# One minimum for both halves of the keys in a softmax, and the division by its sums moved to the gate of the output

## The chip, the cores and the metric

The kernel runs on one core of a Trainium2 chip. The metric is the device time of one execution in microseconds (us); the number given for a kernel is the median of its runs. Beside it stands one execution taken with the hardware profiler, from which all rows below come.

## What is computed

One layer of a bidirectional encoder in float32, for a prompt of 1024 tokens ("p" in the names of tiles) and a sample of 512 ("s"). After a combined input projection two groups of eight heads work side by side: a gated delta rule (group A, a scan in both directions) and a dense attention (group B). Both are multiplied by a gate, put side by side and go through the output projection. The change touches the attention alone:

```python
s = jnp.einsum('bhqd,bhkd->bhqk', qi, k) * MLA_SCALE     # query and key: 128 columns + 64 rotated ones
p = jax.nn.softmax(s, axis=-1)                           # over all positions
o_b = jnp.einsum('bhqk,bhkd->bhqd', p, v)
mix = jnp.concatenate([o_a * jax.nn.silu(z_a), o_b * jax.nn.silu(z_b)], axis=-1)
y = jnp.einsum('bse,ed->bsd', mix, w_out)
```

## The kernel before

Matmuls take float32 operands that are split into a rounded high part and a low part; a product is then three matmuls (high by high, high by low, low by high). `split` (its lines 196 and 199 in the profile) makes the two parts: ScalarE copies the high one, VectorE or POOL subtracts for the low one.

TensorE's order is written out by hand. Every part of the program is a generator that issues some matmuls, adds their estimated time to a clock (`cost`) and yields the time from which it wants to go on. `merge` always lets the first stream go on whose time has come: the three streams of the delta rule (scan, back, front) first, then the main stream, then one that may fill gaps. When none is ready, the clock jumps ahead. The times steer only the order; on the chip TensorE runs that order as fast as operands and buffers allow. The order on the other engines and on SP's DMA queue is found by the compiler's own simulation, beforehand.

In the stretch from 2137 us the main stream is `attention`, first for the prompt, then for the sample. The delta rule's last heads run beside it; when they are done, products of the output projection (`first`, lines 1151 to 1153) may fill gaps. All streams before that end earlier.

`attention` goes over eight heads, for each over blocks of 256 queries. `keys` makes the head's keys, `scores` the scores of one block, `pair_values` the values of two heads. The keys lie in halves of 512: two halves for the prompt (`nh` = 2), one for the sample (`nh` = 1). `scores` takes 128 queries at a time (loop over `i`) and, for each half, writes five matmuls (lines 1013 to 1017) into one of two banks (tile `s`). VectorE finds the minimum of the half (line 1020, the scores are negated), ScalarE the exponential with its sum (line 1021). After the second half the two are brought to a common minimum: a factor for each half, the sum of both, its reciprocal (lines 1029 to 1033), and POOL multiplies the probabilities `pe` by the factor (line 1035). With one half it is a reciprocal (line 1026) and the multiplication. After each half `scores` yields.

`values` works on an earlier block, 256 keys at a time: TensorE transposes the probabilities into the one bank `pt` (line 1074), ScalarE and VectorE split it into `pth` and `ptl` (lines 196 and 199), and `pv` multiplies the parts of the step before by the values into the one bank `po` (lines 1051 to 1053). At the last step of a block VectorE multiplies `po` by the gate `z` (line 1056), and the result goes to DRAM. Between two steps of `values` the planner leaves `PLAT` = 2.0 of its time; `beside` calls one step of `values` after each yield of `scores`, `keys` or `pair_values`, and starts the next half `SLAT` = 3.0 after the one before the last ended.

## Time and profile before

| | |
|---|---|
| median of 3 runs | 3327.83 us (3327.79 to 3335.36) |
| profiled execution | 3330.34 us, span 3328.5 us |
| busy over the span | TensorE 3166.2 us (95%), VectorE 1739.8, ScalarE 1282.5, POOL 1154.3 |
| granted TensorE clock, mean | 0.985 |
| attention over the prompt | 2137 to 2683 us |
| attention over the sample | 2683 to 2850 us |

The span runs from the first to the last instruction. PE is TensorE's matmuls, PEld its weight loads (which run beside the matmuls of the instruction before), DVE is VectorE, ACT ScalarE, POOL GpSimd, SP the queue that issues the DMAs. A busy time is a sum of rows; rows of TensorE overlap, since a matmul's row lasts until its last result is written while the next one has already begun. Idle time stands beside a group of instructions with the operations that ended it.

### The profile page before, as it was taken

What the parts mean: (1) busy time and instruction counts of PE and PEld (TensorE: products, weight loads), DVE (VectorE), ACT (ScalarE), POOL (GpSimd) and SP (SyncE); (2) the same over time, 40 slices, a digit from 0 to 9 for tenths busy, and PEclk for the clock granted to TensorE, in tenths of its full rate; (3) what the DMA queues carried; (4) which work ended last, traced back from release to release, by engine and by line L of the source; (5) the groups of instructions that cost most, each with busy time, mean ns of one, the idle gap of its engine ahead of it and who ended that gap; (6) DMA issues with size and microseconds to landing.
All of it is one profiled execution on the core that took longest, in us unless ns stands there. A gap on an engine that the chain in (4) does not pass through costs nothing.

```text
span 3328.5 us, 46972 instructions
## 1 busy us (share of the span) xinstructions
PE 3166.2 (95%) x16554; PEld 2628.6 (79%) x16554; DVE 1739.8 (52%) x4000; ACT 1282.5 (39%) x2956; POOL 1154.3 (35%) x1026
## 2 busy tenths in 40 slices
PE   8999999999999899999999988899999989999998
PEld 6888888888887678778788767688888878777876
DVE  7233334434411746765775576788787655330212
ACT  4222222222212334444345334365666555433231
POOL 6322222222222543332332333232223434454452
PEclk9999999999999899999999999999999999999999
DMA  4222222222222544434444466522322242564454
GB/s 160 84 70 74 78 73 80 71 79 80 86 73 73 179 119 123 120 107 137 130 109 127 137 209 210 160 82 59 102 77 79 90 134 86 159 189 134 145 171 133
DMA packets 271404, 381.66 MB, mean 115 GB/s; under 512 B 75632, under 2 KB 126824, under 8 KB 269632
## 3 DMA queue, kind: packets, MB, share of 16 engines
q1 hardware_dynamic: 271168, 378.66, 37.3%
q8 instruction: 130, 2.13, 0.3%
q14 instruction: 106, 0.87, 0.1%
HBM read 286.73 MB, written 88.29 MB: 113 GB/s over the span
## 4 chain that ended last, share of the span: by engine, by line
PE 28%; DVE 11%; DMA 7%; issue 3%; ACT 2%; POOL 2%; SPq 1%; POOLq 0%; DVEq 0%; ACTq 0%
DMA wraw<-w_out 3%; PE py L1152 3%; PE py L1151 3%; PE py L1153 3%; POOL wlo L199 2%; PE mm L224 2%; PE pt L1074 2%; PE mm L228 2%; PE mm L225 2%; DVE tm L737 2%; DVE XT L739 1%; PE po L1052 1%; PE po L1051 1%; PE po L1053 1%; PE Tp L791 1%
## 5 line engine op out<-in xcount | busy, mean ns | idle before, releaser
L199 POOL TENSOR_TENSOR wlo<-wraw,whi 128x512 fp32r<-128x512 f32 x620 | 831.7, 1345 | 1593.4 <-ACT whi L196 1476.3
L224 PE MATMUL mm<-hi,whi 128*128 128x512 f32 x2256 | 908.0, 404 | 21.8 <-ACT whi L196 16.3
L225 PE MATMUL mm<-lo,whi 128*128 128x512 f32 x2256 | 883.0, 393 | 8.1 <-DVE lo L255 8.1
L196 ACT ACTIVATE whi<-wraw 128x512 fp32r<-128x512 f32 x620 | 388.7, 631 | 1186.2 <-PE mm L225 695.8
L228 PE MATMUL mm<-hi,wlo 128*128 128x512 f32 x2256 | 765.5, 393 | 4.6 <-POOL wlo L199 4.6
L224 PEld LDWEIGHTS mm<-hi,whi 128*128 128x128 f32 x2256 | 428.1, 190 | 107.6 <-ACT whi L196 18.6
L228 PEld LDWEIGHTS mm<-hi,wlo 128*128 128x128 f32 x2256 | 426.5, 189 | 98.9 <-POOL wlo L199 7.2
L225 PEld LDWEIGHTS mm<-lo,whi 128*128 128x128 f32 x2256 | 427.9, 190 | 92.1 <-DVE lo L255 9.7
L1152 PE MATMUL py<-wlo,mhi 128*128 128x512 f32 x768 | 304.6, 397 | 8.1 <-POOL wlo L199 8.0
L1151 PE MATMUL py<-whi,mhi 128*128 128x512 f32 x768 | 303.7, 395 | 5.9 <-DVE y L1166 4.6
L1153 PE MATMUL py<-whi,mlo 128*128 128x512 f32 x768 | 303.1, 395 | 0.0
L1035 POOL TENSOR_TENSOR pe<-pe,af 128x512 f32<-128x512 f32 x160 | 166.6, 1058 | 373.2 <-DVE af L1033 189.9
L306 DVE SCALAR_TENSOR_TENSOR acc<-cin,conv_w,acc 128x1024 f32<-128x1024 f32 (+1 forms) x192 | 222.3, 1158 | 40.7 <-ACT acc L304 33.6
L302 DVE TENSOR_TENSOR cin<-mm,rbh 128x512 f32<-128x512 f32 x72 | 47.4, 687 | 310.0 <-PE mm L228 261.0
L1152 PEld LDWEIGHTS py<-wlo,mhi 128*128 128x128 f32 x768 | 145.2, 189 | 46.0 <-POOL wlo L199 14.6
L1151 PEld LDWEIGHTS py<-whi,mhi 128*128 128x128 f32 x768 | 145.2, 189 | 40.4 <-DVE y L1166 6.1
L1153 PEld LDWEIGHTS py<-whi,mlo 128*128 128x128 f32 x768 | 145.2, 189 | 32.3
L310 DVE TENSOR_TENSOR acc<-mm,rbh 128x512 f32<-128x512 f32 x48 | 31.6, 686 | 227.9 <-PE mm L228 227.6
L1166 DVE TENSOR_TENSOR y<-py,g 128x512 f32<-128x512 f32 x36 | 24.7, 689 | 239.3 <-ACT junk L1165 236.0
L1021 ACT ACTIVATE pe<-s,am 128x512 f32<-128x512 f32 x160 | 110.4, 690 | 89.1 <-DVE am L1020 78.5
L737 DVE TENSOR_TENSOR tm<-XT,lam 128x126 f32<-128x126 f32 (+22 forms) x372 | 131.2, 353 | 25.3 <-ACT lam L729 18.5
L199 DVE TENSOR_TENSOR ptl<-pt,pth 128x512 fp32r<-128x512 f32 x160 | 109.8, 686 | 52.7 <-ACT pth L196 51.8
(449 smaller groups left out, 5133.5 us busy)
## 6 DMA issues: line engine op xcount, KB each, us to landing
wraw<-w_in SPq DMA_DIRECT2D x376, 256.0 KB
wraw<-w_out SPq DMA_DIRECT2D x192, 256.0 KB
dd<-dX SPq DMA_DIRECT2D x48, 256.0 KB
wraw<-w_uq SPq DMA_DIRECT2D x36, 256.0 KB
x<-xT_p SPq DMA_DIRECT2D x16, 512.0 KB
xres<-x_p SPq DMA_DIRECT2D x8, 1024.0 KB
y_p<-y SPq DMA_DIRECT2D x32, 256.0 KB
x<-xT_s SPq DMA_DIRECT2D x16, 256.0 KB
```

The costliest lines, as they stand in the source:

```text
L196: nc.scalar.activation(hi, src, AF.Copy)
L199: (lo_eng or nc.vector).tensor_sub(lo, src, hi.bitcast(F32))
L224: nc.tensor.matmul(ps, whi[:, k], hi[:, s], start=kt == 0, stop=False)
L225: nc.tensor.matmul(ps, whi[:, k], lo[:, s], start=False, stop=False)
L228: nc.tensor.matmul(ps, wlo[:, k], hi[:, s], start=False, stop=kt == KT - 1)
L306: nc.vector.scalar_tensor_tensor(acc, cin[:, j:j + T], w[:, f, j:j + 1], acc, op0=ALU.mult, op1=ALU.add)
L737: nc.vector.tensor_mul(tv, XT[:, :m, j:j + 1].to_broadcast([P, m, n]), lam[j // 16][:, j % 16:j % 16 + 1, j + 1:].to_broadcast([P, m, n]))
L1021: nc.scalar.activation(pe[k], o, AF.Exp, bias=m[:, k:k + 1], scale=-1.0, accum_out=l[:, k:k + 1])
L1035: nc.gpsimd.tensor_mul(pe[k2], pe[k2], f[:, k2:k2 + 1].to_broadcast([P, BLK]))
L1151: nc.tensor.matmul(ps, hi[:, c], w[0], start=kt == kts[0], stop=False)
L1152: nc.tensor.matmul(ps, hi[:, c], w[1], start=False, stop=False)
L1153: nc.tensor.matmul(ps, lo[:, c], w[0], start=False, stop=kt == kts[1] - 1)
```

## The change

For the prompt, both halves of the scores are now written before anything else follows. The minimum of both halves goes into both exponentials, so that the halves need no factor. The probabilities stay undivided. Per block of 256 queries VectorE adds up the sums of the halves and takes the reciprocal; a DMA writes these 256 numbers to a row in DRAM, another reads the row back to all partitions (`rb`), and POOL multiplies the gate `z` by it before the gate is used. The planner gets a new constant `HLAT` = 2.4 after a pair of halves, and calls two steps of `values` after each pair (and after each yield of `keys` and `pair_values` for the prompt). For the sample, with one half, the order of `scores` and `values` stays.

```diff
@@ -29,6 +29,7 @@
 GAP = 8
 PLAT = 2.0
 SLAT = 3.0
+HLAT = 2.4
 
 
 QKV0, ZA0, CQ0, CKV0, ZB0, LAST = 0, 24, 32, 36, 38, 46
@@ -950,6 +951,7 @@
                     nc.vector.tensor_sub(krl[:64, ks], r[:64], krs[:64, ks].bitcast(F32))
         for h in range(H):
             self.dt(f"mix{8 + h}{q}", [P, T])
+        self.dt("rl" + q, [H, T])
 
         bank = lambda name: pss.tile([P, BLK], F32, tag="s", name=name, bufs=2)
 
@@ -987,7 +989,7 @@
                 yield
             out[:] = [vh, vl]
 
-        def scores(h, kh, kl, t0, pes):
+        def scores(h, kh, kl, t0, pes, rls):
             tq = slice(t0, t0 + QB)
             qn = ap.tile([P, QB], F32, tag="qn", name="qn")
             qp = ap.tile([P, QB], F32, tag="qp", name="qp")
@@ -1000,12 +1002,12 @@
             qr = ap.tile([P, QB], F32R, tag="qr", name="qr", bufs=2)
             nc.scalar.activation(qr, qp, AF.Copy)
             nc.vector.tensor_sub(qr[64:], qp[64:], qr[64:].bitcast(F32))
+            l = sm.tile([P, QB // P, nh], F32, tag="al", name="al", bufs=3)
+            rl = sm.tile([P, QB // P], F32, tag="ar", name="ar", bufs=4)
             for i in range(QB // P):
                 qs = slice(i * P, (i + 1) * P)
-                pe = []
+                pe, os = [], []
                 m = sm.tile([P, nh], F32, tag="am", name="am", bufs=4)
-                l = sm.tile([P, nh], F32, tag="al", name="al", bufs=4)
-                f = sm.tile([P, nh], F32, tag="af", name="af", bufs=4)
                 for k in range(nh):
                     ks = slice(k * BLK, (k + 1) * BLK)
                     pe.append(ap.tile([P, BLK], F32, tag="pe", name="pe", bufs=8 if nh > 1 else 6))
@@ -1016,25 +1018,27 @@
                     nc.tensor.matmul(o, qr[:, qs], krs[:, ks], start=False, stop=False)
                     nc.tensor.matmul(o, qr[:, qs], krl[:, ks], start=False, stop=True)
                     self.cost(BLK, 5)
+                    os.append(o)
 
                     nc.vector.tensor_reduce(m[:, k:k + 1], o, axis=AX.X, op=ALU.min)
-                    nc.scalar.activation(pe[k], o, AF.Exp, bias=m[:, k:k + 1], scale=-1.0,
-                                         accum_out=l[:, k:k + 1])
-                    if k == nh - 1:
-                        mm = sm.tile([P, 1], F32, tag="amm", name="amm", bufs=4)
-                        if nh == 1:
-                            nc.vector.reciprocal(f, l)
-                        else:
-
-                            nc.vector.tensor_tensor(mm, m[:, 0:1], m[:, 1:2], op=ALU.min)
-                            nc.scalar.activation(f, m, AF.Exp, bias=mm, scale=-1.0)
-                            nc.vector.scalar_tensor_tensor(l, l, 1.0, f, op0=ALU.mult, op1=ALU.mult, accum_out=mm)
-                            nc.vector.reciprocal(mm, mm)
-                            nc.vector.tensor_scalar(f, f, mm, None, op0=ALU.mult)
-                        for k2 in range(nh):
-                            nc.gpsimd.tensor_mul(pe[k2], pe[k2], f[:, k2:k2 + 1].to_broadcast([P, BLK]))
-                    yield
+                    if k < nh - 1:
+                        yield True
+                mm = m
+                if nh > 1:
+                    mm = sm.tile([P, 1], F32, tag="amm", name="amm", bufs=4)
+                    nc.vector.tensor_tensor(mm, m[:, 0:1], m[:, 1:2], op=ALU.min)
+                for k, o in enumerate(os):
+                    nc.scalar.activation(pe[k], o, AF.Exp, bias=mm, scale=-1.0, accum_out=l[:, i, k:k + 1])
                 pes.append(pe)
+                if i == QB // P - 1:
+
+                    src = l[:, :, 0]
+                    if nh > 1:
+                        nc.vector.tensor_reduce(rl, l, axis=AX.X, op=ALU.add)
+                        src = rl
+                    nc.vector.reciprocal(rl, src)
+                    rls.append(rl)
+                yield
 
 
         past, done, tick = [0.0, 0.0], [0.0], [0]
@@ -1046,12 +1050,17 @@
                 b["po"] = ps1.tile([P, QB], F32, tag="po", name="po")
                 b["z"] = ap.tile([P, QB], F32, tag="az", name="az", bufs=2)
                 nc.sync.dma_start(b["z"], S[f"f{ZB0 + b['h']}{q}"][:, b["tq"]])
+                nc.sync.dma_start(S["rl" + q][b["h"]:b["h"] + 1, b["tq"]].rearrange("a (i p) -> p (a i)", p=P), b["rl"][0])
             po, z = b["po"], b["z"]
             for j in range(2):
                 nc.tensor.matmul(po, vh[:, kb + j], hi[:, j], start=kb + j == 0, stop=False)
                 nc.tensor.matmul(po, vh[:, kb + j], lo[:, j], start=False, stop=False)
                 nc.tensor.matmul(po, vl[:, kb + j], hi[:, j], start=False, stop=kb + j == nt - 1)
             self.cost(2 * QB, 3)
+            if kb == 0:
+                rb = cp.tile([P, BLK], F32, tag="raw", name="rlb")[:, :QB]
+                nc.sync.dma_start(rb, S["rl" + q][b["h"]:b["h"] + 1, b["tq"]].to_broadcast([P, QB]))
+                nc.gpsimd.tensor_mul(z, z, rb)
             if kb + 2 == nt:
                 nc.vector.tensor_mul(z, po, z)
                 nc.sync.dma_start(S[f"mix{8 + b['h']}{q}"][:, b["tq"]], z)
@@ -1086,15 +1095,22 @@
             done[0] = self.t
 
         def beside(gen):
+            part = 0
             while True:
-                yield max(self.t, past[0] + SLAT)
+
+                yield self.t if part else max(self.t, past[1] + HLAT if nh > 1 else past[0] + SLAT)
                 try:
-                    next(gen)
+                    half = next(gen)
                 except StopIteration as e:
                     return e.value
                 past[:] = past[1], self.t
                 tick[0] += 1
+                part = part + 1 if half else 0
+                if part:
+                    continue
                 yield from values()
+                if nh > 1:
+                    yield from values()
 
         def finish():
             while queue or now[0] is not None or last[0] is not None:
@@ -1107,13 +1123,13 @@
                 wk = self.piece(a["w_uk"][h // 2], nc.gpsimd, ap, "2", 2, rb=3 - nh)
             kh, kl = yield from beside(keys(h % 2, wk))
             for t0 in range(0, T, QB):
-                pes = []
-                yield from beside(scores(h, kh, kl, t0, pes))
+                pes, rls = [], []
+                yield from beside(scores(h, kh, kl, t0, pes, rls))
                 if h % 2 == 0 and t0 == 0:
                     yield from finish()
                     wv = self.piece(a["w_uv"][h // 2], nc.gpsimd, ap, "2", 2, rb=3 - nh)
                     yield from beside(pair_values(wv, vs))
-                queue.append({"h": h, "tq": slice(t0, t0 + QB), "pes": pes, "tick": tick[0] + LAG,
+                queue.append({"h": h, "tq": slice(t0, t0 + QB), "pes": pes, "rl": rls, "tick": tick[0] + LAG,
                               "vs": [v[:, :, h % 2 * P:(h % 2 + 1) * P] for v in vs]})
         yield from finish()
```

## Rows read from the trace of the kernel before

**Rows 1.** The page: busy us of each engine, share of the span, instructions.

```profile
PE 3166.2 (95%) x16554; PEld 2628.6 (79%) x16554; DVE 1739.8 (52%) x4000; ACT 1282.5 (39%) x2956; POOL 1154.3 (35%) x1026
```

**Rows 2.** Stretches: length; busy us of PE, PEld, DVE, ACT, POOL; clock; DMA.

```profile
2137.00:2683.00 546.00, 512.53 (x3524) 445.96 (x3523) 424.34 (x1238) 325.95 (x910) 165.85 (x162) 0.99 0.28 84
2300.00:2500.00 200.00, 189.85 (x1400) 168.26 (x1399) 168.04 (x512) 120.77 (x354) 54.72 (x54) 1.00 0.27 80
```

**Rows 3.** Groups by line, 2137:2683: busy us, mean ns | idle before, releasers.

```profile
L1074 PE MATMUL pt<-ident,pe 128*128 128x128 f32 x512 | 80.0, 277 | 19.9 <-DVE ptl L199 10.2 <-DVE amm L1029 3.2 <-POOL pe L1035 2.4
L1074 PEld LDWEIGHTS pt<-ident,pe 128*128 128x128 f32 x512 | 59.6, 141 | 38.0 <-issue 12.4 <-DVE ptl L199 10.3 <-POOL pe L1035 4.4
L1013 PE MATMUL s<-kh,qh 128*128 128x512 f32 x128 | 54.4, 425 | 4.9 <-ACT pe L1021 2.6 <-DVE vl L199 2.3
L199 DVE TENSOR_TENSOR ptl<-pt,pth 128x512 fp32r<-128x512 f32 x128 | 87.8, 686 | 40.7 <-ACT pth L196 40.3
```

**Rows 4.** Timeline of PE, one half step alone: start us, us, instruction.

```profile
2497.67 0.40 PE L1013 MATMUL s<-kh,qh 128*128 128x512 f32 x1
...
2498.60 0.40 PE L1017 MATMUL s<-krl,qr 128*128 128x512 f32 x1
2498.84 0.60 PE L1074 MATMUL pt<-ident,pe 128*128 128x128 f32 x4
...
2499.99 0.39 PE L1013 MATMUL s<-kh,qh 128*128 128x512 f32 x1
```

**Rows 5.** Timeline of PE at a stalled transposition group (idle in brackets).

```profile
2404.42 0.40 PE L1017 MATMUL s<-krl,qr 128*128 128x512 f32 x1
2406.21 0.66 PE L1074 MATMUL pt<-ident,pe 128*128 128x128 f32 x4 [1.39 <-DVE ptl L199]
```

**Rows 6.** Groups by line, 2683:2850, the shorter attention.

```profile
L1074 PE MATMUL pt<-ident,pe 128*128 128x128 f32 x128 | 19.4, 274 | 2.2 <-DVE ptl L199 2.2
...
L1074 PEld LDWEIGHTS pt<-ident,pe 128*128 128x128 f32 x128 | 15.5, 140 | 7.8 <-DVE ptl L199 4.3
```

**Rows 7.** Groups by line, 2137:2683, operations that the change removes.

```profile
L1035 POOL TENSOR_TENSOR pe<-pe,af 128x512 f32<-128x512 f32 x128 | 132.6, 1057 | 322.7 <-DVE af L1033 189.9 <-PE pt L1074 22.5 <-DVE XT L739 14.9
L1030 ACT ACTIVATE af<-am,amm 128x2 f32<-128x2 f32 x64 | 19.2, 300 | 5.1 <-DVE amm L1029 4.5
L1033 DVE TENSOR_SCALAR af<-af,amm 128x2 f32<-128x2 f32 x64 | 15.3, 239 | 3.1 <-DVE XT L739 0.2
L1031 DVE SCALAR_TENSOR_TENSOR al<-al,af 128x2 f32<-128x2 f32 x64 | 11.0, 172 | 4.5 <-ACT af L1030 4.0
```

**Rows 8.** Timeline of POOL and DVE at one of the multiplications.

```profile
2401.68 2.04 POOL L1035 TENSOR_TENSOR pe<-pe,af 128x512 f32<-128x512 f32 x2 [7.43 <-PE s L1014]
2402.72 1.28 DVE L199 TENSOR_TENSOR ql<-qn,qh 128x256 fp32r<-128x256 f32 x1
```

**Rows 9.** Tile qn, whole span: duration ns min/median/max, first and last start.

```profile
L199 DVE TENSOR_TENSOR ql<-qn,qh x48: 411/425/1327, 2141.6 to 2816.8; 128x256 fp32r<-128x256 f32 x48
```

**Rows 10.** Timeline of DVE and ACT in the stretch of rows 4.

```profile
2499.04 0.69 DVE L1020 TENSOR_REDUCE am<-s 128x1 f32<-128x512 f32 x1 [0.23 <-PE s L1017]
2499.48 0.60 ACT L196 ACTIVATE pth<-pt 128x512 fp32r<-128x512 f32 x1 [1.72 <-PE pt L1074]
2499.97 0.68 ACT L1021 ACTIVATE pe<-s,am 128x512 f32<-128x512 f32 x1
2500.11 0.69 DVE L199 TENSOR_TENSOR ptl<-pt,pth 128x512 fp32r<-128x512 f32 x1 [0.38 <-ACT pth L196]
```

**Rows 11.** Timeline of PE: scores of half steps with no other work, first, last.

```profile
2180.07 0.40 PE L1013 MATMUL s<-kh,qh 128*128 128x512 f32 x1
...
2585.26 0.40 PE L1013 MATMUL s<-kh,qh 128*128 128x512 f32 x1
```

**Rows 12.** Chain of work that ended last: start us, us, landing of a write.

```profile
2159.57 1.89 DMA dUs<-UA
...
2680.70 1.73 DMA mix15p<-az
```

## Prediction

> **What bounds the kernel now.** I read first the page's busy times: TensorE is busy 95% of the span [rows 1], so a change that touches no matmul can only win back TensorE's waits. The question is how many lie where the change acts: the attention over the prompt (2137 to 2683 us) and the shorter one behind it (2683 to 2850). The table by stretches comes next: in the prompt attention TensorE is busy 512.5 of 546 us and VectorE 424.3, in its middle 168.0 of 200 [rows 2]. VectorE is the next to fill up.
>
> Third, the groups by line. TensorE's idle time ahead of the transpositions of the probabilities (tile pt, line 1074) is 19.9 us in its matmul row and 38.0 us in the row of its weight loads, of which 12.4 is put down to issue; the largest named releaser of both is VectorE's ptl (10.2 and 10.3). Ahead of the scores it is 4.9 us [rows 3]. The true figure lies between: a matmul of 512 columns has a row of 0.40 us but the next starts 0.23 us after it [rows 4], so a wait shows in the matmul row only when the pipeline has run dry. Counting in the timeline how much later than 0.23 us a transposition group starts, I get 28 us over the 128 groups, as at 2406.21 us, where 1.79 us lie between the starts and 1.56 are lost [rows 5]. In the shorter attention the same rows say 2.2 and 7.8 us [rows 6]; there I take 3. Everything that can be won at this spot is thus some 31 us, 0.9% of the time.
>
> **The change, part by part.** Taken away in the prompt attention: 128 POOL multiplications (132.6 us), 64 exponentials of the two-column factor on ScalarE (19.2 us), and on VectorE the product of sums and factors (11.0 us) and the scaling (15.3) [rows 7]. Of 64 reciprocals 32 stay, one per block of 256 queries, and with each comes a reduction of 4 columns to 2. The trace has none of that size; by the nearest row, two columns in 172 ns [rows 7], 32 cost 5.5 us, about what the 32 reciprocals save. So VectorE is relieved of some 11.0 + 15.3 = 26 us, 6% of its 424. POOL gets 48 multiplications of 128x256, half the width of those of 1057 ns: about 0.53 us each, 25 us over both attentions, on an engine that is busy 35% [rows 1]. None of this is on TensorE, so by itself it is worth nothing; it counts only where a wait of TensorE ends on VectorE or POOL.
>
> There is a second relief. At 2401.68 POOL runs two of the multiplications, 2.04 us; VectorE's ql takes 1.28 us beside them [rows 8], where its median is 425 ns [rows 9]. With POOL's 132.6 us gone most of this stretching goes too. I bound it from 0 to 30 us of VectorE time (128 times at most a quarter of a microsecond) and put VectorE's relief at 26 to 56 us, 6 to 13%.
>
> The order on TensorE changes as well. Before, each half of the scores is followed by a transposition group and a product group. After: both halves of the scores, then twice (transpositions, products), because the exponentials need the minimum of both halves. What follows for the single transposition buffer is read from a stretch without other work. One half step is 2.32 us: scores from 2497.67, transpositions from 2498.84, the next scores at 2499.99; transpositions and products take 1.15 us together [rows 4]. The transpositions of 2498.84 are copied by ScalarE from 2499.48 for 0.60 us, and ptl runs from 2500.11 for 0.69, done at 2500.80 [rows 10]. So the buffer is free 1.96 us after the group began. Before, the next group comes after 2.32 us, 0.36 to spare. After, the first group of a pair comes 1.15 + 2.33 = 3.48 us behind its predecessor, 1.5 to spare, the second only 1.15 us: it waits 1.96 - 1.15 + 0.04 (from ptl's end to the next matmul) = 0.85 us where nothing stands between. The planner puts 2.0 us of its own time between two such groups and fills them from the delta rule or the output projection; a scan item ready every 2.1 planned us is nearly always there. In the timeline 22 of 128 half steps hold nothing else, the first without a wait at 2180.07, the last at 2585.26 [rows 11], so I take 11 bare pairs (8 to 16).
>
> The sum for the prompt attention: of 28 us of waits the half before first groups goes, -14. The 53 covered second groups keep 14 x 53/64 = 11.6 less a quarter for VectorE's relief, 8.7; 11 bare ones cost 9.4 (7 to 14). Left are 18, gain 10. The 2.4 us that transpositions wait for POOL [rows 3] go.
>
> Against it: the next scores need a bank back. After the last matmul of a pair has begun come the second minimum (0.44 later, 0.69 long), the minimum of the two halves (two columns, 0.17) and the first exponential (0.68) [rows 4, 7, 10]: 1.98 us and two hand-overs of some 0.04. TensorE has meanwhile that matmul's 0.23 and two groups of 1.15, 2.5 us. It holds, by 0.5 us. Waits for a bank are 4.9 us now [rows 3]; I add 2 (0 to 6). Behind the first block of each second head the values' product follows a pair directly: four times up to 2 us, +1 (0 to 8).
>
> **The round trip of the sums.** Per block two DMAs come onto SP's queue: 256 sums of 4 bytes each to DRAM, then one row broadcast to all partitions, which waits for the first to land. The gate's multiplication on POOL waits for the second, behind it the low parts of weights, and VectorE's final product of the block waits for POOL. The nearest rows: a write of a block's result lands in 1.73 us, the 64 KB of dU, in 128-byte pieces, in 1.89 [rows 12]. Two landings and the multiplication are some 4.3 us, with two issues 5. From the products' first group, where the sums are issued at the latest, to the last there are three transposition groups, in the prompt attention some 9 us. Cover: those groups. Cost zero; without cover it would be the part beyond.
>
> The shorter attention (one half of keys) keeps its order, loses 32 POOL multiplications and 16 of 32 reciprocals: its 3 us of waits become 2, -1. Sum: -9.9 - 2.4 + 2 + 1 - 1 = -10.3 us. The span of 3328.5 becomes 3318.2; the profiled execution took 3330.3, 1.8 more than its span and 2.5 more than the median 3327.8. Against the median: 3327.8 - 10.3 = **3317.5 us**.
>
> **The rivals.** (a) *Slower: ScalarE takes the exponentials first.* The order of its queue is fixed beforehand. If the new exponential, ready 1.2 us after a pair, stands ahead of the copy of the first transposition group, ready at 0.65, the copy and with it ptl come a whole exponential (0.68) and the wait for it (0.5) later. Bare pairs then lose 0.85 + 1.18 = 2.0 us each, 22 in all, and covered ones about 0.3, 16: 38 us stand where 28 stood, with the 3 for banks and values +13, 3341. It decides from a mean wait of 28/64 = 0.44 us before second groups on. For it: VectorE's and ScalarE's waits show many places where a fixed order did not fit the chip (ptl's idle time of 40.7 us ends nearly always on ScalarE's pth [rows 3]). Against it: pth is ready first.
> (b) *No change: waits only move.* Bank waits grow by 6, the values' by 4, and bare pairs are 16 (14 us): 28 become 8.7 + 14 = 22.7, so -5.3 - 2.4 + 6 + 4 - 1 = +1, with smaller shares between 3323 and 3332.
> (c) *More is won.* If the waits at ptl come from VectorE's crowding alone, a relief of 13% ends most covered waits, too: 28 become 10, the bank waits don't grow and the shorter attention gives 3: -18 - 2.4 - 4 - 3 = -27, 3301. The Trainium skill, "Perfetto Trace Analysis", section "Identifying the Most-Contended Engine", judges TensorE by its weight loads and not by its matmul row, which is pipelined. Here that row shows 79% [rows 1], and by its 38.0 and 7.8 us of idle [rows 3, 6] the sum would be nearer to this case.
> (d) *The round trip is late*: the last product of a block waits, VectorE with it. If each landing takes twice 1.89 us, the 5 become 8.8, the whole of the 9; where the planner runs groups closer some 0.5 us is missing, and with VectorE blocked behind it that is 8 us if it meets a third of the 48 blocks and 24 if it meets all, on top of the forecast: 3325 to 3341. The Trainium skill, "DMA: Bandwidth & Descriptors", section "Rules for kernel authors", says that a strided last dimension is lowered to one descriptor per element, which speaks against this write; no row here shows 4-byte pieces.
>
> **How the numbers follow.** A repeat of this kernel tells about 0.3%, 10 us, from no change: bounds 3318 and 3338. Forecast (3310 to 3323, likeliest 3317.5) 0.44, of which two thirds lie beyond 10 us; (a) (3338 to 3348) 0.20; (b) 0.20; (c) (3296 to 3308) 0.11; (d) 0.05. Faster: 0.29 + 0.11 = 0.40. Same: 0.15 + 0.20 + 0.03 = 0.38. Slower: 0.20 + 0.02 = 0.22. The range reaches into (c) and (a) to about their middles, which leaves out 0.16: 3302 to 3342.
>
> **What would show it.** In the profile after, idle time before line 1074 should be 15 to 20 us in the prompt attention, nearly all of it at second groups, with ptl as releaser; VectorE's busy time there should fall by 30 to 55 us and POOL's by over 100; ql should keep near 425 ns. If pth's rows start after the exponentials of the same pair, (a) is right. If the scores wait over 8 us for the exponentials, (b). If VectorE's last product of a block waits for POOL, (d). The sum is wrong altogether if the planner's new spacing leaves many more bare pairs than 16, or if the gain sits in a stretch before 2137 us or after 2850 us.

## The result, and the profile after

The changed kernel takes 3581.6 us (median of 4 runs, 3577.7 to 3587.8), the kernel before 3327.8: ratio 1.076, 95% interval 1.0741 to 1.0779. That is 254 us slower, 240 above the upper end of the predicted range. The profiled execution took 3583.9, its span is 3582.1. Below, each ratio is against the kernel before on the same chip, and 1% is 33.3 us.

From the page of after: busy us, share and instructions of each engine, then the groups of the gate's multiplication and of the transpositions (busy, mean ns | idle time before, releaser).

```profile
PE 3239.7 (90%) x16554; PEld 2690.3 (75%) x16554; DVE 1709.7 (48%) x3792; ACT 1268.9 (35%) x2892; POOL 1021.8 (29%) x914
...
L1063 POOL TENSOR_TENSOR az<-az,rlb 128x256 f32<-128x256 f32 x48 | 35.4, 737 | 796.3 <-DMA rlb<-rlp 325.3
L1083 PE MATMUL pt<-ident,pe 128*128 128x128 f32 x640 | 106.8, 293 | 122.8 <-DVE ptl L200 122.6
```

Beside [rows 1] the work went as the diff says: VectorE 30 us less, POOL 133 less, as many matmuls. TensorE's busy time is still 73.5 us longer, at a mean granted clock of 0.955 in place of 0.985, and its share falls from 95% to 90%: the rest of the time was added as waits. Their largest place is the line that was to win, ahead of the transpositions: 122.8 us of idle time over both attentions, where [rows 3, 6] have 19.9 + 2.2.

By stretches (length; busy us of PE, PEld, DVE, ACT, POOL; clock; DMA share and GB/s), the attention over the prompt and the one over the sample, and below them the sample's in the kernel before:

```profile
2137.00:2850.00 713.00, 577.20 (x3672) 501.96 (x3671) 403.91 (x1052) 326.41 (x872) 73.09 (x79) 0.92 0.30 76
2850.00:3117.00 267.00, 186.97 (x846) 154.36 (x844) 81.05 (x150) 81.92 (x184) 39.17 (x38) 0.81 0.32 68
```
```profile
2683.00:2850.00 167.00, 158.79 (x873) 134.32 (x872) 90.78 (x168) 85.90 (x188) 71.73 (x61) 0.98 0.37 109
```

The prompt's attention has grown from 546 us [rows 2] to 713 (with 148 more matmuls in it), the sample's from 167 to 267, although its order of scores and values is the old one. What the two have in common is the round trip of the sums. Its waits, by queue and engine, whole span (us in total, times, longest):

```profile
SPq L1062 <- DMA rlp<-ar: 230.9, 32, 8.3
SPq L1062 <- DMA rls<-ar: 117.9, 16, 8.8
```

At each of the 48 blocks SP's queue stands 7.3 us on average at the read, because the write has not landed. VectorE's own wait for the gate, first from 2137 to 2850 us, then from 2850 to 3117:

```profile
DVE az L1065 <- POOL az L1063: 15.7, 6, 3.9
```
```profile
DVE az L1065 <- POOL az L1063: 52.0, 10, 8.5
```

So in the prompt VectorE waits in 6 blocks of 32 only. There the write goes out 5.6 us before the block's first product group, and the last group begins 11.8 us after the first (medians); in the sample it is 4.4 and 5.1 us. One block of the prompt on SP and on POOL (start, us):

```profile
2294.13 0.39 SPq L1053 DMA_DIRECT2D rlp<-ar  x1
2302.06 0.33 SPq L1062 DMA_DIRECT2D rlb<-rlp  x1
```
```profile
2307.78 0.73 POOL L1063 TENSOR_TENSOR az<-az,rlb 128x256 f32<-128x256 f32 x1 [21.97 <-issue]
```

Write issued to read issued 7.9 us, read issued to POOL's start 5.7: 13.7 us to the start of the multiplication, where the prediction had some 5 to its end. And a block of the sample, with TensorE and VectorE:

```profile
2940.28 0.36 PE L1056 MATMUL po<-pth,vh 128*128 128x256 f32 x1
...
2946.90 0.58 PE L1056 MATMUL po<-pth,vh 128*128 128x256 f32 x1 [3.82 <-ACT pth L197]
```
```profile
2943.16 0.53 SPq L1053 DMA_DIRECT2D rls<-ar  x1
2951.10 0.33 SPq L1062 DMA_DIRECT2D rlb<-rls  x1
```
```profile
2956.70 0.42 DVE L1065 TENSOR_TENSOR az<-po,az 128x256 f32<-128x256 f32 x1 [8.53 <-POOL az L1063]
...
2962.74 1.11 PE L1083 MATMUL pt<-ident,pe 128*128 128x128 f32 x4 [7.25 <-DVE ptl L200]
```

A block of the sample has two product groups, not four. Of this block, the one with the longest wait, the first began at 2940.28, the second, the last, at 2946.90. VectorE, whose next instruction in order is the product with the gate, stands 8.53 us until 2956.70. The ptl copy lies behind it, and TensorE's transpositions come at 2962.74, idle for 7.25. But the gate is not the last wait there: ptl starts 4.87 us after the gate's product has ended. Before it can copy pth, ScalarE stands in its fixed order at two loads of the next queries:

```profile
2957.55 0.42 ACT L197 ACTIVATE qh<-qn 128x256 fp32r<-128x256 f32 x1 [8.57 <-DMA qn<-q4s]
...
2960.39 0.42 ACT L1003 ACTIVATE qr<-qp 128x256 fp32r<-128x256 f32 x1 [2.42 <-DMA qp<-qr2s]
...
2961.99 0.69 DVE L200 TENSOR_TENSOR ptl<-pt,pth 128x512 fp32r<-128x512 f32 x1 [0.32 <-ACT pth L197]
```

SP issued these loads at 2952.48 and 2957.59 only, behind the read and behind the next gate's load, which waited for a result to land. The chain that ended last has both ways in it (start, us):

```profile
3028.56 8.15 DMA rls<-ar
...
3036.73 5.11 DMA rlb<-rls
...
3042.06 0.73 POOL az L1063
...
3042.82 0.43 DVE az L1065
3043.25 0.53 SPq L1053
...
3043.82 8.11 DMA qp<-qr3s
```

A write and its read hold up the gate; then a load of queries, issued right behind the next write (L1053), takes 8.1 us. In the block above such a load, issued at 2958.09 just ahead of a write, was there at 2960.39.

### The profile page after: what moved, and what is told of

It reads as the page before. It is cut to its first block, busy times and chain, and to the rows that moved or that the text cites. A ratio compares the mean times of both kernels' runs of the same rounds, so it can differ in the third digit from the quotient of the medians.

```text
span 3582.1 us, 46499 instructions
## 1 busy us (share of the span) xinstructions
PE 3239.7 (90%) x16554; PEld 2690.3 (75%) x16554; DVE 1709.7 (48%) x3792; ACT 1268.9 (35%) x2892; POOL 1021.8 (29%) x914
## 5 line engine op out<-in xcount | busy, mean ns | idle before, releaser
L226 PE MATMUL mm<-lo,whi 128*128 128x512 f32 x2256 | 884.3, 393 | 10.1 <-DVE lo L256 10.1
L1063 POOL TENSOR_TENSOR az<-az,rlb 128x256 f32<-128x256 f32 x48 | 35.4, 737 | 796.3 <-DMA rlb<-rlp 325.3
L1083 PE MATMUL pt<-ident,pe 128*128 128x128 f32 x640 | 106.8, 293 | 122.8 <-DVE ptl L200 122.6
L1083 PEld LDWEIGHTS pt<-ident,pe 128*128 128x128 f32 x640 | 81.7, 150 | 148.8 <-DVE ptl L200 114.3
```

What stands on the lines that cost most here:

```text
L226: nc.tensor.matmul(ps, whi[:, k], lo[:, s], start=False, stop=False)
L1083: nc.tensor.transpose(pt[:, j, i * P:(i + 1) * P], b["pes"][i][k][:, c:c + P], self.ident)
```

## The experiments

**Trip or order.** Two halves of the change, each alone. First the change without the round trip (the write, the read and the gate's multiplication left out, so nothing divides):

```diff
-                nc.sync.dma_start(S["rl" + q][...].rearrange("a (i p) -> p (a i)", p=P), b["rl"][0])
...
-                nc.sync.dma_start(rb, S["rl" + q][...].to_broadcast([P, QB]))
-                nc.gpsimd.tensor_mul(z, z, rb)
```

> The changed kernel without the round trip: the two DMAs of the sums and the multiplication of the gate are left out, so the output stays undivided; order, minimum and sums are as changed. Theory T (the round trip through DRAM costs the time: SP waits 230.9 + 117.9 us for the sums to land and VectorE's last product of a block waits for the gate): 3310 to 3335 us, waits of TensorE before the transpositions back under 40 us. Rival O (the order in pairs, with its short second step, costs the time): over 3500 us. If both have a share it falls between, and the distance to 3328 is the order's share.

Measured: 3369.1 us, ratio 1.0127 (1.0110 to 1.0144), between the two forecasts. Then the kernel before with the same round trip added (its probabilities are divided as before and the gate once more):

> The kernel before, in its own order and with its own factors and multiplications on POOL, with only the round trip added: the reciprocals are written to DRAM, read back to all partitions and multiplied into the gate (which then divides twice). T: 3450 to 3620 us, SP waits 7 to 8 us for each of 48 writes. O: 3325 to 3345 us.

Measured: 3508.0, ratio 1.0545 (1.0510 to 1.0580). So the trip costs 7.60 - 1.27 = 6.33%, 211 us, in the new order and 181 in the old; the rest of the change costs 42 by itself, where 10 were to be won. The run without a trip ends the prompt's last products at 2743 us and the sample's at 2913, the change at 2837 and 3114: of the trip's cost some 90 us lie in the prompt's 32 blocks and 107 in the sample's 16.

**The pieces.** The write as one row of 1 KB (one query's probabilities in place of the sums), and as 128 pieces of 8 bytes, read back in that order:

```diff
-  nc.sync.dma_start(S["rl" + q][...].rearrange("a (i p) -> p (a i)", p=P), b["rl"][0])
+  nc.sync.dma_start(S["rl" + q][...], b["pes"][0][0][0:1, :QB])
```

> The change with the write of the sums replaced by a write of one contiguous row of 1 KB (256 probabilities of one query, so that the gate is multiplied by other values); the read, the wait of its issue and the multiplication stay. Theory L (the landing is long because of the 256 pieces of 4 bytes): the write lands in about 1.8 us as a block's result does, the read's issue is held 1 to 1.5 us and not 7.3, the trip takes 7 to 8 us and not 13.7, and the time is 3380 to 3450. Rival (two DMAs that depend on each other on one queue take this long whatever their pieces): 3560 to 3600, the read's issue still held 7 us.

```diff
-  ....rearrange("a (i p) -> p (a i)", p=P), b["rl"][0])
+  ....rearrange("a (p i) -> p (a i)", p=P), b["rl"][0])
```

> The change with the sums laid down as 128 pieces of 8 bytes in place of 256 of 4 (the row in DRAM has another order, and POOL reads it back in that order). If the landing time goes with the number of pieces, the read's issue is held about 4.2 us in place of 7.3 (1.8 plus half of what is beyond, less the time to the read), and the time is 3480 to 3550. If the landing is long for any write of pieces this small, whatever their number: 7 us still, 3570 to 3590.

Measured: one row 3382.9, ratio 1.0175 (1.0140 to 1.0210); 128 pieces 3426.7, ratio 1.0307 (1.0282 to 1.0331). SP's hold at the read, first of the one row, then of the 128 pieces:

```profile
SPq L1062 <- DMA rlp<-pe: 19.3, 23, 2.1
```
```profile
SPq L1062 <- DMA rlp<-ar: 83.5, 31, 3.9
```

In the prompt's 32 blocks the queue is held 231, 84 and 19 us with 256, 128 and 1 pieces; over the run without a trip the time is 6.3, 1.8 and 0.5% longer (the interval of the last overlaps that of the run without a trip). The length of the trip comes from the number of pieces. With 128 it cost less than the expectation had (1.8 where 3.3 was its lower end): the cost rises faster than the count. A shorter trip is covered in more of the blocks: VectorE's wait for the gate is 10.1 us in 4 blocks there, 67.7 in 16 in the change.

**By which way the length reaches TensorE.** Four runs on that. First the gate used late: POOL multiplies behind VectorE's product, so that VectorE waits for nothing:

```diff
-                nc.gpsimd.tensor_mul(z, z, rb)
...
                 nc.vector.tensor_mul(z, po, z)
+                nc.gpsimd.tensor_mul(z, z, b["rb"])
```

> The changed kernel, but the reciprocals meet the result after VectorE's last product of a block (on POOL, before the write of the result), so that VectorE never waits for the read-back; both DMAs stay on SP's queue. If the cost goes through VectorE's wait for the gate (T1): under 3400 us. If it goes through SP's queue, which holds loads and writes back while it waits for the sums to land (T2): over 3500 us.

Measured: 3443.7, ratio 1.0351 (1.0327 to 1.0376), between the two: late use takes 4.1 of the 6.3%. But the hold of SP fell with it (108 us in the prompt), so it didn't part the two theories. A version with the read later (at the third group of a prompt block, the second of a sample block) and the result sent off in the next block was to take both waits away:

```diff
-            if kb == 0:
+            if kb + 2 == nt // 2 + 2:
                 nc.sync.dma_start(rb, ...)
...
+        def flush():            # called at kb == 0 of the next block
+                nc.gpsimd.tensor_mul(b["z"], b["z"], b["rb"])
+                nc.sync.dma_start(S[f"mix{8 + b['h']}{q}"][:, b["tq"]], b["z"])
```

> The change as it is, with the round trip spread out: the sums are written at the first product group of a block as before, read back only at the third (prompt) or second (sample), and the gate's row is multiplied behind VectorE's product, at the beginning of the next block, where the result is also sent off. Neither SP's queue nor VectorE then stands waiting for a landing. Theory T1+T2 (the 212 us of the trip are VectorE's wait for the gate and SP's queue held behind the read, and nothing else): close to the run without a trip, 3369, at most 20 more: 3365 to 3390. Rival (the small pieces or the extra transfers disturb other DMAs or engines by being there): over 3420.

Measured: 3455.7, ratio 1.0394 (1.0375 to 1.0414). The rival's number; but SP was still held 113 us at the prompt's reads, for the queue's order, found beforehand, had put them up close behind the write. Then the whole trip on POOL's queue, first with the early gate, then with the late one and the result's write there too:

```diff
-  nc.sync.dma_start(S["rl" + q]..., b["rl"][0])
+  nc.gpsimd.dma_start(S["rl" + q]..., b["rl"][0])
...
-  nc.sync.dma_start(rb, S["rl" + q]...)
+  nc.gpsimd.dma_start(rb, S["rl" + q]...)
```

> The change as it is, but both transfers of the round trip are issued from POOL's queue in place of SP's. SP's queue is no longer held behind the read; VectorE still waits for the gate. If VectorE's wait is the whole way (T1): within 30 us of the change, ratio 1.065 to 1.085. If the held queue is the whole way (T2): ratio 1.012 to 1.025, as without a trip. If both carry a part: between, in the share of VectorE's wait.

> The change with the whole round trip on POOL's queue (the write of the sums, the read of the row, the multiplication behind VectorE's product, and the write of the block's result): neither SP's queue nor VectorE stands waiting for a landing, and the 256 pieces of 4 bytes are still written. If the two waits are all that the trip costs: ratio 1.012 to 1.020, as without a trip (1.013). If the small pieces by themselves disturb the other transfers: 1.03 and more.

Measured: 1.0745 (1.0714 to 1.0776) and 1.0458 (1.0427 to 1.0488). With SP free at the read nothing is won; but POOL's queue stands there in its place (321 us in the first run, 190 in the second), so these two runs alone don't rule out the held queue. The late use, with the result sent off from POOL's queue, is worth 2.9% here, 96 us. And 3.3% remain although VectorE doesn't wait for the gate and SP not at the read. SP does wait at the next gate's load, 319 us over both attentions where it is 49 without a trip, for results that go out behind the trip. (This run's page counts 48 packets under 512 bytes for each block where the change has 288, so the pieces can't be counted on this queue.) What else is left shows in the second run's trace; POOL, SP and ScalarE at a block of the sample:

```profile
2881.58 0.73 POOL L1053 DMA_DIRECT2D rls<-ar  x1
...
2891.28 0.54 POOL L1062 DMA_DIRECT2D rlb<-rls  x1 [6.06 <-DMA rls<-ar]
```
```profile
2883.03 0.38 SPq L996 DMA_DIRECT2D qn<-q4s  x1
```
```profile
2895.90 0.42 ACT L197 ACTIVATE qh<-qn 128x256 fp32r<-128x256 f32 x1 [16.89 <-DMA qn<-q4s]
```

The load of the next queries, issued 1.5 us behind the write on another queue, is there 12.9 us later. In the kernel before, ScalarE waits 0.9 us for this tile in the whole span. Two loads of weights were issued between the two, so the row alone doesn't say what delays it. So a third theory: while the small pieces are under way, other transfers land late, whoever waits. The test is the write alone, with nobody reading it and no division:

```diff
             if kb == 0:
-                rb = cp.tile(...)
-                nc.sync.dma_start(rb, S["rl" + q]...)
-                nc.gpsimd.tensor_mul(z, z, rb)
```

> The change with the write of the 256 sums alone: nobody reads the row, nothing waits for the write, the gate is not multiplied (the probabilities' sums divide nothing). It differs from the run without a trip by 48 writes of 256 pieces of 4 bytes. Theory T3 (while such a write is under way the transfers issued behind it land late, whoever waits): what the run with everything late on POOL's queue kept beyond the run without a trip stays, ratio 1.030 to 1.050. Rival (only what waits for the write counts): 1.011 to 1.018, as without a trip (1.013).

Measured: 3496.5, ratio 1.0501 (1.0484 to 1.0519). Writes that nobody reads cost 3.7%, 124 us. Over both attentions SP waits 229 us for blocks' results, 49 in the run without a trip, and ScalarE 55 us for loads of queries, 4 in that run. SP at one of these writes, then SP's wait for that result:

```profile
2851.11 0.58 SPq L1053 DMA_DIRECT2D rls<-ar  x1
2851.79 0.41 SPq L1062 DMA_DIRECT2D mix8s<-az  x1
2852.30 0.37 SPq L207 DMA_DIRECT2D wraw<-w_out  x1
2862.94 0.32 SPq L1052 DMA_DIRECT2D az<-f39s  x1
```
```profile
SPq L1052 <- DMA mix8s<-az: 12.8, 2, 10.2
```

A block's result (mix8s) issued right behind the write is not landed until 2862.9, 11 us after its issue, one of the longest, where one in [rows 12] took 1.73; the next gate's load waits for it, and SP with it. The DMA engines are not full meanwhile: from 2853 to 2863 us their share is 0.13. Nor is it SP's wait for the sums at the write itself: that is 20 us here, and 135 us with the one row, which cost 0.5%. The parts don't add up neatly. The late use on SP's queue (2.2% over no trip) costs less than the write alone. SP waits 74 us for results there and not 229, which would fit a hold at the read that keeps other transfers from being issued behind the pieces; this was not tested. Of the 211 us, the late transfers thus take 75 to 124 and the early use of the gate with the read 87 to 136, by which run one subtracts. VectorE's wait itself is 68 us by its rows.

**The order.** The kernel before in its own order, with the work left out that the change takes away (no factors, no sums combined, no division, no multiplication on POOL):

```diff
-                    if k == nh - 1:
-                        mm = ...
-                        ...
-                            nc.gpsimd.tensor_mul(pe[k2], pe[k2], f[:, k2:k2 + 1].to_broadcast([P, BLK]))
                     yield
```

> The kernel before in its own order (each half of the scores followed by a transposition and a product group), with the work taken away that the change takes away and nothing added: no factors, no combined sums, no reciprocals, no multiplication of the probabilities on POOL (so the halves are neither brought to a common minimum nor divided). The run without the round trip had the same relief in the order of the change and took 3369, 44 us more than before. Theory O (the order costs it: the second group of a pair waits for the one buffer pt): with the old order the relief shows by itself, some 10 us of the 28 us of waits, 3305 to 3322. Rival R (the relief itself costs, by the other order that it brings on VectorE, ScalarE and POOL): 3345 to 3370. By the prediction's sum the relief is worth 2.4 us for POOL and a quarter of the waits, 7: 3315.

And the order of the change with each half's own minimum, without a trip:

```diff
                     nc.vector.tensor_reduce(m[:, k:k + 1], o, axis=AX.X, op=ALU.min)
+                    nc.scalar.activation(pe[k], o, AF.Exp, bias=m[:, k:k + 1], ...)
...
-                for k, o in enumerate(os):
-                    nc.scalar.activation(pe[k], o, AF.Exp, bias=mm, ...)
```

> The run without the round trip, in the order of the change (both halves of the scores, then twice transpositions and products), but each half takes its own minimum, so that its exponential follows its scores as before, and no factor brings the halves together and nothing divides. It differs from the run with the relief alone (3302) only in TensorE's order, and from the run without a trip (3369) only in what the exponentials wait for. Theory S (the order of the groups alone costs): 3355 to 3372. Rival M (the common minimum costs, by exponentials that come late and in a heap, behind which copies stand): 3305 to 3330.

Measured: relief alone 3302.3, ratio 0.9938 (0.9918 to 0.9959), 21 us won; in the new order with own minima 3357.7, ratio 1.0083 (1.0066 to 1.0100). The spacing of the groups costs 1.45%, 48 us; the common minimum the 0.44% from there to the run without a trip, 15 us. The relief alone leaves out more than the change does, the reciprocals too (VectorE is busy 1678.4 us, 1698.7 with own minima, 1707.3 without a trip). So 21 us is more relief than the change has, and the 48 us hold 80 small VectorE operations besides the order.

Where: counting each transposition group's late start in the timeline of the run without a trip, as in [rows 5], the 54 groups with scores ahead of them wait 2.0 us in all, the 62 second groups with other work ahead 18.6, the 11 bare ones 22.6, 2.05 each on average (0.86 to 5.7). By the same count the kernel before has 22.5 in all, the relief alone 17.3. A bare one (PE, DVE and ACT together):

```profile
2282.15 0.60 PE L1078 MATMUL pt<-ident,pe 128*128 128x128 f32 x4
...
2282.60 0.69 DVE L1023 TENSOR_REDUCE am<-s 128x1 f32<-128x512 f32 x1
...
2282.79 0.60 ACT L197 ACTIVATE pth<-pt 128x512 fp32r<-128x512 f32 x1
...
2283.21 0.29 DVE L740 TENSOR_TENSOR XT<-XT,tm 128x133 f32<-128x133 f32 x1
2283.53 0.42 DVE L1004 TENSOR_TENSOR qr<-qp,qr 64x256 fp32r<-64x256 f32 x1
...
2283.98 0.16 DVE L1029 TENSOR_TENSOR amm<-am 128x1 f32<-128x1 f32 x1
2284.06 0.68 DVE L200 TENSOR_TENSOR ptl<-pt,pth 128x512 fp32r<-128x512 f32 x1
...
2284.80 0.66 PE L1078 MATMUL pt<-ident,pe 128*128 128x128 f32 x4 [1.33 <-DVE ptl L200]
```

ScalarE copies at once (pth 0.64 after the group's start, done 2283.39), but VectorE still has the pair's minimum, an operation of the scan, one of the next queries and the common minimum in its fixed order, so ptl begins 0.67 us late. The second group starts 2.65 after the first in place of 1.15.

Whether a divided buffer would help was tried, without a trip, with the bank's two halves copied apart:

```diff
-                pt = ps1.tile([P, 2, QB], F32, tag="pt", name="pt")
+                    pt = ptb[:, j]          # one tile for all, halves j = 0, 1
...
+                    self.split(hi[:, j], lo[:, j], pt)
```

> The run without the round trip, with the transpositions' one bank used as two halves of 256 columns that are copied and freed apart (twice as many copies of half the size on ScalarE and VectorE). Theory B (a second group of a pair waits because the one buffer comes free only after both copies of the whole): bare second groups wait under 0.6 us in place of 2.05, the time is 3340 to 3358. Rival C (ScalarE and VectorE are late with the copies whatever the buffer, because of their other work): more instructions make it no better, 3365 to 3390.

Measured: 3659.8, ratio 1.0993 (1.0971 to 1.1014). PE, DVE and ACT at the second half of a group:

```profile
2250.78 0.38 ACT L197 ACTIVATE pth<-pt 128x256 fp32r<-128x256 f32 x1
2251.20 0.42 DVE L200 TENSOR_TENSOR ptl<-pt,pth 128x256 fp32r<-128x256 f32 x1 [3.54 <-ACT pth L197]
2251.68 0.69 PE L1081 MATMUL pt<-ident,pe 128*128 128x128 f32 x2 [3.11 <-DVE ptl L200]
```

The second half's transpositions wait for the first half's ptl: the two halves of the one tile were ordered as one buffer, so each group makes the round to ScalarE and VectorE twice. TensorE's wait for ptl rose from 36.8 us in the run without a trip to 232.7. This says nothing on two true buffers, which were not tried.

**Versions without the pieces.** A division on TensorE with no trip at all: the transposition becomes a product with the reciprocals on a diagonal.

```diff
-  nc.tensor.transpose(pt[...], b["pes"][i][k][:, c:c + P], self.ident)
+  nc.tensor.matmul(pt[...], b["pes"][i][k][:, c:c + P], b["rl"][i], start=True, stop=True)
```

> The changed kernel without round trip and without multiplication of the gate: the division sits in the matmul that transposes the probabilities, whose identity is replaced by a diagonal of the reciprocals (two products of 128x128 on VectorE per block). T: 3310 to 3335 us, as without the trip, plus at most some 10 us for 96 more operations of VectorE. O: over 3500 us.

Measured: 3436.5, ratio 1.0329 (1.0310 to 1.0348), 67 us over the run without a trip. TensorE ran 1280 instructions in place of 640, and its busy time is 73.5 us longer (3252.6 against 3179.1):

```profile
L1083 PEld LDWEIGHTS pt<-dgs,pe x1280: 186/192/338, 2175.6 to 2974.5; 128*128 128x128 f32 x183
L1083 PE MATMUL pt<-dgs,pe x1280: 270/275/583, 2175.8 to 2974.7; 128*128 128x128 f32 x183
```

Last, a cheap trip: VectorE transposes the reciprocals in squares of 32x32, and 8 pieces of 128 bytes go out when they are ready. Once in the change itself, once in the old order with a factor for the first half only (the second takes the minimum of both, so POOL multiplies 64 times and not 128):

```diff
+  nc.vector.transpose(rt, rl)                      # rl: 128 x 32, two columns used
+  row = S["rl" + q][h:h + 1, tq].rearrange("a (i b c) -> (a i) b c", b=4, c=32)
+  for j in range(QB // P):
+      nc.sync.dma_start(row[j], rt[j:P:32])
...
   nc.vector.tensor_mul(z, po, z)
+  nc.gpsimd.tensor_mul(z, z, b["rb"])
```

> The change with its pairs of halves and its common minimum, and with the same cheap trip: the reciprocals transposed on VectorE and written as 8 pieces of 128 bytes as soon as they are there, read back at the first product group, multiplied on POOL behind VectorE's product. If the pieces were the cost of the trip: close to the run without a trip (3369), 3365 to 3385, so that only the order's 44 us stay. If two dependent transfers cost beyond their pieces: 3400 and more.

> A version put together from what the runs showed: the order before (a transposition and a product group behind each half). The second half takes the minimum of both, so that only the first half's probabilities need a factor on POOL (64 multiplications in place of 128), and the division goes to the gate. The 256 reciprocals are first transposed on VectorE in squares of 32x32, so that they go to DRAM as 8 pieces of 128 bytes; the row is read back at the first product group, and POOL multiplies the block's result by it behind VectorE's product. Theory (order and pieces were the whole cost, the relief is real): half of the 22 us that the run with the relief alone won, less up to 5 us for the cheap trip: 10 us faster than before, ratio 0.995 to 1.000, some 3308 to 3320 beside a kernel before of 3324. Rival (a round trip costs even with few pieces, 14 us and more as with the one row): ratio 1.000 to 1.008.

Measured: the change with the cheap trip 3383.0, ratio 1.0157 (1.0141 to 1.0173), 10 us over no trip; the old order 3320.2, ratio 0.9969 (0.9957 to 0.9982), 10 us faster than before and the one version with the division that beats both kernels. From the latter's page and its tile of transposed reciprocals:

```profile
PE 3164.2 (95%) x16554; PEld 2628.2 (79%) x16554; DVE 1729.2 (52%) x3968; ACT 1281.7 (39%) x2956; POOL 1093.0 (33%) x978
```
```profile
L1035 DVE STREAM_TRANSPOSE art<-ar x48: 199/211/214, 2164.5 to 2822.5; 128x32 f32<-128x32 f32 x48
```

48 transpositions of 211 ns, 10 us of VectorE, take the place of 12,288 pieces.

## Why the prediction was wrong

**The step that failed is "Cover: those groups. Cost zero".** Of its three terms one was mis-sized, one held for the prompt alone, and one was put at nothing.
- The landing. I priced 256 pieces of 4 bytes by the 1.89 us of dU's 128-byte pieces [rows 12], though no row showed such pieces; it took 7.9 (8.3 in the median of the 48). The upper bound, twice 1.89, was a guess dressed as a bound: the number of pieces had been counted and not used. The sentence of the Trainium skill quoted there against the write, "DMA: Bandwidth & Descriptors", section "Rules for kernel authors", was right: the run with the write alone has 13,056 more packets under 512 bytes than the one without, 272 for each of the 48. Rival (d), in whose text it stands, was given 0.05.
- The cover. The 9 us were those of a prompt block, three groups, and there it was larger than I had it: with the write 5.6 us ahead of the first group and 11.8 us from the first group to the last, VectorE waited in 6 blocks of 32 although the trip took 13.7. A sample block has two groups, so one step lies between them, 2.8 us in the kernel before (median of 16). By my reckoning a third of the 48 blocks had no cover even for the 5 us that I had. They lost most: 107 us in 16 blocks, against some 90 in 32.
- Who else pays. I let VectorE wait for the gate (rival (d): 0.5 us at each block; measured 68 us in 16 waits over both attentions, the longest 8.5), and never asked what the write does to the transfers beside it: that term was nothing, without a reason. It is 75 to 124 us. The Trainium skill, "DMA: Bandwidth & Descriptors", section "Queues, rings and completion order", says that a transfer's completion mark lands only after every earlier write of the same DMA engine; the result that landed 11 us after its issue, behind the pieces, agrees. The Trainium skill, "DMA: Bandwidth & Descriptors", section "Issuing engines are not separate DMA queues", says that the engine which issues makes no difference to where the transfers run; the run on POOL's queue, 1.0745 against 1.0760, agrees.

**The named sign was there.** "If VectorE's last product of a block waits for POOL, (d)": it did, in 16 of the 48 blocks. (d) stood in the text with a ceiling of 24 us for that wait; its rows have 68, and the runs put 87 to 136 of the 211 us on the early use of the gate with the read. The late transfers, the other part, (d) did not have.

**The order.** Count and sign of the parts were right, one size was not. First groups of a pair lost their waits (2.0 us left; the forecast's -14). Eleven bare second groups, as predicted, but 2.05 us each and not 0.85: that figure came from a half step in which VectorE was free [rows 10], and after a pair it is not. 0.85 is the least: the best bare pair lost 0.86. Covered second groups wait 18.6 and not 8.7. Waits at pt thus rose from 22.5 to 43.2 where I had them fall from 28 to 18; the other late starts of that stretch (delta rule, values, banks) rose by some 26 more, of which my terms held 3. Rival (a), ScalarE's exponentials first, was not the cause in most pairs: pth starts on average 0.6 us behind the start of its group's last transposition. Its total of 22 us for bare pairs came out all the same, by VectorE: the number was luck. Rival (c)'s sum takes 4 us off for bank waits of which its text says only that they don't grow.

**The relief.** Undersized: 2.4 for POOL and a quarter of the waits, some 9 us, against 21 measured with the order kept, though with twice VectorE's saving of the change (61 us and not 30). VectorE's 30 us over the whole span are about what the left-out operations took; of the 0 to 30 us of stretching nothing shows. ql kept its median of 425 ns as said, and its longest too (1327 before). POOL saved what was listed, but its 48 multiplications of the gate took 35.4 us and not 25.

```profile
L200 DVE TENSOR_TENSOR ql<-qn,qh x48: 415/425/1312, 2143.2 to 3064.3; 128x256 fp32r<-128x256 f32 x48
```

Sum by the runs: relief -21, spacing +48, common minimum +15, round trip +211: +253, of 254 measured between the medians.

## What to carry to other kernels

Count the pieces of a transfer, not its bytes, and look for a row with such pieces; if there is none, the price is open upwards, and the bound must be worked from the count. Price a transfer also by what it does to those issued behind it, even if nobody waits for it itself, and ask for its cover in every stage and shape in which it runs, the shortest first. And a spacing that is right with an idle helper engine is not right just behind the work that loads that engine: take the time of a copy from the place in the order where it will stand.

## What the hardware showed

- A write of 256 pieces of 4 bytes to DRAM landed in 7.9 us (8.3 in the median of 48), one of 128 pieces of 8 bytes in about 3.6 (issue at 2291.27, dependent read at 2294.86), one row of 1 KB in 1.1 (2405.76, 2406.87). All 256 packets of such a write have begun 1.4 us after its issue (median), most with a row of 9 ns; in the sample block above, while its landing was awaited, the DMA engines moved nothing (the row of 2946 us below ends with clock, DMA share and GB/s). What the rest of the landing time goes to, no run here shows. Transfers issued behind such a write landed up to 11 us after their issue in the run with the write alone.
- A float32 product of 128x128 with a diagonal takes two instructions per matmul on TensorE where the transposition takes one: 640 more, and a run 67 us longer. The Trainium skill, "Perfetto Trace Analysis", section "Transposes", asks for transpositions in place of matmuls; these rows agree.
- The granted clock fell with the waits: 0.98 to 0.81 in the sample's attention. After the 3.82 us of idle time ahead of 2946.90 TensorE ran at the lower of its two levels, 1.2 GHz (granted 0.54 from 2946 to 2953 us), and at 2.4 again from 2953.47 on. The stretch, then rows of one shape (128x512) at either level:

```profile
2946.00:2953.00 7.00, 5.96 (x19) 4.78 (x19) 1.46 (x3) 1.63 (x5) 0.00 (x0) 0.54 0.00 0
```
```profile
2950.14 0.63 PE L1018 MATMUL s<-krs,qr 128*128 128x512 f32 x1
...
2953.47 0.40 PE L967 MATMUL kp<-cl,whi 128*128 128x512 f32 x1
```

So a wait costs twice: the idle time, and the slower matmuls behind it.
